# A decoder layer on one core: three quarters of the MLP's down projection as seven block products instead of eight, interleaved with the next up projections

## The chip, the core and the metric

The kernel runs on one core of a Trainium2 chip. The core has a matrix engine (TensorE, PE in the profile; its weight loads are PEld), a vector engine (VectorE, DVE), a scalar engine (ScalarE, ACT), a small general engine (GpSimd, POOL) and a queue engine (SyncE, SP) that issues most transfers from memory. Each engine works through its own list of instructions in order and waits for the others by semaphores. The metric is the device time of one execution in microseconds (us).

## What is computed

One layer: a normalised input projection, two token mixers, an output projection, then the MLP, then a gated side input. Only the MLP and its neighbours change:

```python
h  = h + rmsnorm(mixed @ w_o, g_post_mix)
v2 = rmsnorm(h, g_pre_mlp)
f  = jnp.square(jax.nn.relu(v2 @ w_up)) @ w_down      # w_up 1024x4096, w_down 4096x1024
h  = h + rmsnorm(f, g_post_mlp)
gate = jax.nn.sigmoid(rmsnorm(h, g_pre_ple) @ w_ple_gate + b_ple_gate)
h  = h + rmsnorm(gate * (p @ w_ple_in), g_post_ple)
```

There are 512 tokens (`S`), 1024 features (`D`) and 4096 hidden features (`FF`), all in 32-bit floats.

## The kernel before, in words

A matrix product of two 32-bit operands is made of three matmuls: each operand is split into a rounded part and the rest (`split`: ACT rounds, then DVE subtracts), and `PASSES` lists hi·hi, hi·lo, lo·hi. A matmul is 128x128 against 128x512.

Weights come in units of 256 rows by 512 columns (512 KB, one tile of the pool `pt`, 24 buffers, called `t`). `loads` fixes the order of the transfers on SP, `plan` the order in which `prep_next` splits units into the ring `w` of five buffers; `take` hands them to PE in the same order. A sixth unit is split only once the first has been used.

MLP before: the hidden features are cut into eight blocks of 512. `up()` computes one block as `gemm(4, feed(vT), ..., wstat=True)`: four units, 96 matmuls into four banks `a`, one for each 128 hidden features; ACT takes relu and square, DVE the rest of the split. Then for each half `n` of the output `gemm(2, list_feed(f_j), tok_out(facc, n, ...))` adds the block's share to `facc`: 48 matmuls for a half, 96 for a block. The order is up 0, up 1, down 0, up 2, down 1, and so on; the last block's down product is in the closing loop, which also makes the residual sum (`residual_features`: DVE, ACT, the power on POOL in `rstd`, then transposes `to_features` on PE).

The retention heads already use a seven-product form (`quartet`, Strassen-Winograd): a product of 2x2 blocks done as the products "11", 1, "12", 2, 4, 7, "22", whose operands are sums of the blocks. It has seven products of 24 matmuls in place of eight; `add_quartet` plans the sums of the weights.

`h1` (the residual, four tiles) and `e` (the side input's projection, two pairs of tiles) stay in the pool through the whole MLP. Tiles are written here as the listings print them: `t` pool tiles, `w` split weights, `u` the normalised, transposed activations (`vT`, `hT`), `s` half tiles, `a` and `b` banks, `st` and `rs` statistics.

Of the kernel before, what the change touches and what calls it, by code (L numbers as in the profile page):

```python
# [10 lines left out]
F32 = mybir.dt.float32  # L11
F32R = mybir.dt.float32r
# [12 lines left out]
MAGIC = 12582912.0  # L25
TWO_PI = (6.25, 17 / 512, -37 / 2 ** 21, 2 * math.pi - (6.25 + 17 / 512 - 37 / 2 ** 21))
PI_IN = 3.1415925
N_RAW, N_W, N_T, N_S = 4, 5, 24, 12


@with_exitstack
def hybrid_block(ctx, tc, a, out):
# [38 lines left out]
    def split(hi, lo, src):  # L71
        act(hi, src)
        tt(lo, src, hi.bitcast(F32), OP.subtract)
# [27 lines left out]
    def pop():  # L101
        if not raws:
            load_next()
        return raws.pop(0)
# [20 lines left out]
    def add_quartet(w, n1, n2):  # L125
        x, y, z = {}, {}, {}

        def first(k):
            x[k] = pop()
            return x[k]  # L130

        def add(a, b):
            tt(a, a, b, OP.add)
            return a

        def t1(k):
            y[k] = pop()
            return add(x[k], y[k])

        def t2(k):  # L140
            z[k] = pop()
            return add(x[k], z[k])

        for f, n, k0 in ((first, n1, 0), (t1, n2, 0), (lambda k: pop(), n1, 2), (t2, n2, 2),
                         (lambda k: z[k], None, 0), (lambda k: add(y[k], z[k]), None, 0),
                         (lambda k: add(x[k], pop()), n1, 2)):
            for k in range(2):
                if n is not None:
                    loads.append(w[n, k0 + k])
                plan.append(lambda f=f, k=k: f(k))  # L150

    w_in, w_ro, w_do = a["w_in"], a["w_ret_out"], a["w_dil_out"]
    for g in range(NG):
# [3 lines left out]
        add_units(w_in, c)  # L157
    for h in range(H):
        add_units(w_in, 3 * h)
        add_quartet(w_in, 3 * h + 2, 3 * h + 1)  # L160
    for n in range(2):
        add_units(w_do, n)
    for h in range(H):
# [3 lines left out]
        add_units(a["w_o"], n)  # L167
    add_units(a["w_ple_in"], 0)
    NFC = FF // 512
    add_units(a["w_up"], 0)  # L170
    for j in range(NFC):
        if j + 1 < NFC:
            add_units(a["w_up"], j + 1)
        for n in range(2):
            add_units(a["w_down"][j], n)
    add_units(a["w_ple_in"], 1)
# [172 lines left out]
    posr = half()  # L349

    def rotary(i):
        sc_i = const.tile([P, 2, S], F32, name="rot1") if i else big((P, 2, S))
# [275 lines left out]
    def quartet(lefts, c11, c12, c21, c22, early, late):  # L628
        def product(name, ps, first):
            for kk in range(2):  # L630
                w, = take(1)
                for t in range(2):
                    for k2 in range(2):
                        k = 2 * kk + k2
                        for q, (i, j) in enumerate(PASSES):
                            nc.tensor.matmul(ps[t], lefts[name](k, i, t), w[:, j, k2],  # L636
                                             start=(first and k == 0 and q == 0), stop=(k == 3 and q == 2),
                                             skip_group_check=not first)
# [4 lines left out]
        pa, pc = [abank() for _ in range(2)], [abank() for _ in range(2)]  # L643
        p1, q, u2 = ([half() for _ in range(2)] for _ in range(3))
        product("11", pa, True)
        for t in range(2):
            with tc.high_priority():
                act(p1[t], pa[t])
        product(1, pc, True)
        for t in range(2):  # L650
            with tc.high_priority():
                tt(q[t], pc[t], p1[t], OP.subtract)
        early()
        product("12", pa, False)
        for t in range(2):
            c11(t, pa[t])
        pb = [bank() for _ in range(2)]
        product(2, pb, True)
        for t in range(2):
            with tc.high_priority():  # L660
                tt(u2[t], pb[t], p1[t], OP.add)
        product(4, pc, False)
        for t in range(2):
            with tc.high_priority():
                tt(u2[t], pc[t], u2[t], OP.subtract)
            c12(t, u2[t])
        product(7, pb, False)
        for t in range(2):
            with tc.high_priority():
                tt(q[t], q[t], pb[t], OP.subtract)  # L670
            c22(2 + t, q[t])
        late()
        product("22", pb, False)
        for t in range(2):
            tt(p1[t], pb[t], p1[t], OP.add)
            c21(2 + t, p1[t])

    def rope_pair(x1, x2):
        res = []
# [14 lines left out]
    def head(h):  # L694
# [54 lines left out]
        def gate(t, br):  # L749
            stt(sg[t], br[0], br[1], sg[t])  # L750

        quartet(quads, g_evac, v_evac, g_inner, v_evac, scores,
                lambda: [gate(t, retain(t)) for t in range(2)])
        for t in (2, 3):
            gate(t, retain(t))

# [86 lines left out]
    pT32 = big((P, 2, 512))  # L843
    load(pT32, a["p"])
    pT = []
    for k in range(2):
        o = big((P, 2, 512), F32R)
        split(o[:, 0], o[:, 1], pT32[:, k])
        pT.append(o)

    g_post = bcast(a["g_post_mix"])
    g_pre = bcast(a["g_pre_mlp"])
# [10 lines left out]

    rs1 = const.tile([P, NT], F32, name="rs1")
    r0, ssq = {}, {}

    def wo_first(t, ps):
        ssq[t] = sumsq(ps)
# [19 lines left out]
    def e_evac(n):  # L888
        return lambda t, ps: act(at(e[n], t), ps)

    gemm(1, list_feed(pT), e_evac(0))
    flush()

    facc = [big() for _ in range(NT)]

    def up():
        fs = []

        def f(t, ps):
            r = half()  # L900
            act(r, ps, AF.Relu)
            o = big((P, 2, 512), F32R)
            act(o[:, 0], r, AF.Square)
            tt(r, r, r, OP.mult)
            tt(o[:, 1], r, o[:, 0].bitcast(F32), OP.subtract)
            fs.append(o)
        gemm(4, feed(vT), f, wstat=True)
        return fs
# [11 lines left out]
    rs2 = const.tile([P, NT], F32, name="rs2")  # L920
    us = take(4)
    hT = new_u()
    for t in range(NT):
        parts = []
        for n in range(2):
            ps = abank()
            acc_tile(ps, us[2 * n:2 * n + 2], list_feed(fs[NFC - 1]), t, False, prep_next if t == 3 else None)
            tok_out(facc, n)(t, ps)
            f = facc[t][:, halves[n]]
# [6 lines left out]
        residual_features(t, h1[t], r, g_pre2, rs2[:, t:t + 1], hT, [facc[t][:, sl] for sl in halves], 8)  # L936

    gemm(1, list_feed(pT), e_evac(1))
    flush()

    b_ple = bcast(a["b_ple_gate"])
# [107 lines left out]
```

## Time and profile before

| what | value |
|---|---|
| median of 3 runs | 1253.37 us (1252.58 to 1253.73) |
| the profiled execution's own time | 1251.57 us |
| its span, first to last instruction | 1249.8 us |
| TensorE busy | 1228.3 us, 98% of the span |
| VectorE busy | 746.2 us, 60% |
| ScalarE busy | 554.0 us, 44% |
| GpSimd busy | 50.3 us, 4% |

The span leaves 1.8 us of the profiled execution outside. The busy shares are means over stages; what counts is which engine a stage ends with. A matmul's recorded duration (about 390 ns) is longer than the step from one to the next, since matmuls overlap: a stretch's length divided by its matmuls gives the step.

### The profile page before, as it was taken

What the parts mean: (1) busy time and instruction counts of PE and PEld (TensorE: products, weight loads), DVE (VectorE), ACT (ScalarE), POOL (GpSimd) and SP (SyncE); (2) the same over time, 40 slices, a digit from 0 to 9 for tenths busy, and PEclk for the clock granted to TensorE, in tenths of its full rate; (3) what the DMA queues carried; (4) which work ended last, traced back from release to release, by engine and by line L of the source; (5) the groups of instructions that cost most, each with busy time, mean ns of one, the idle gap of its engine ahead of it and who ended that gap; (6) DMA issues with size and microseconds to landing.
All of it is one profiled execution on the core that took longest, in us unless ns stands there. A gap on an engine that the chain in (4) does not pass through costs nothing.

```text
span 1249.8 us, 15078 instructions
## 1 busy us (share of the span) xinstructions
PE 1228.3 (98%) x5708; PEld 1002.5 (80%) x5708; DVE 746.2 (60%) x1180; ACT 554.0 (44%) x926; POOL 50.3 (4%) x88
## 2 busy tenths in 40 slices
PE   7999999999999999999999999999999999999997
PEld 6877777877777888888888788878888888888886
DVE  6743644553369959769597267574344444354785
ACT  7334444446765535445355332353432233233462
POOL 1002011000010000000000000010000000000010
PEclk9999999999999999999999999999999999999999
DMA  9332233262316332423455343631222423232411
GB/s 339 136 106 72 66 91 112 60 202 70 116 60 227 114 124 92 143 84 135 135 185 200 114 176 120 251 118 34 71 81 86 133 84 101 85 117 72 149 51 68
DMA packets 51561, 149.43 MB, mean 120 GB/s; under 512 B 8352, under 2 KB 8608, under 8 KB 51488
## 3 DMA queue, kind: packets, MB, share of 16 engines
q1 hardware_dynamic: 41184, 133.91, 31.9%
q10 hardware_dynamic: 9024, 13.48, 3.4%
q0 software_dynamic: 1280, 1.08, 0.3%
q8 instruction: 45, 0.74, 0.2%
q14 instruction: 28, 0.23, 0.1%
HBM read 133.18 MB, written 11.53 MB: 116 GB/s over the span
## 4 chain that ended last, share of the span: by engine, by line
PE 92%; DVE 3%; DMA 2%; ACT 1%; issue 1%; POOL 0%; DVEq 0%; POOLq 0%; ACTq 0%
PE a L223 70%; PE a L636 7%; PE b L636 5%; PE b L454 2%; PE b L744 2%; PE b L484 2%; PE b L472 1%; DVE t L69 1%; PE b L729 1%; ACT s L66 1%; DMA t<-in_xT_dram 1%; DMA t<-in_x_dram 1%; DVE t L273 1%; PE b L760 0%; PE b L296 0%
## 5 line engine op out<-in xcount | busy, mean ns | idle before, releaser
L223 PE MATMUL a<-u,w 128*128 128x512 f32 x2112 | 506.7, 395 | 1.3 <-DVE s L69 0.9
L223 PEld LDWEIGHTS a<-u,w 128*128 128x128 f32 x2112 | 390.3, 188 | 87.0 <-issue 4.0
L66 ACT ACTIVATE w<-t 128x1024 fp32r<-128x1024 f32 (+1 forms) x230 | 238.6, 1044 | 263.7 <-PE a L223 187.8
L69 DVE TENSOR_TENSOR w<-t,w 128x1024 fp32r<-128x1024 f32 (+1 forms) x230 | 273.9, 1202 | 110.3 <-ACT w L66 107.7
L223 PE MATMUL a<-w,t 128*128 128x512 f32 x1008 | 231.7, 390 | 0.0
L223 PEld LDWEIGHTS a<-w,t 128*128 128x128 f32 x1008 | 188.8, 188 | 39.0
L69 DVE TENSOR_TENSOR t<-a,t 128x512 f32<-128x512 f32 x112 | 83.0, 743 | 96.4 <-PE a L223 65.0
L69 DVE TENSOR_TENSOR t<-t,t 128x512 f32<-128x512 f32 (+3 forms) x134 | 125.2, 955 | 3.9 <-ACT s L66 2.5
L223 PE MATMUL a<-w,u 128*128 128x512 f32 (+1 forms) x504 | 117.8, 389 | 5.0 <-ACT w L66 5.0
L223 PE MATMUL a<-t,w 128*128 128x512 f32 x480 | 110.5, 391 | 1.0 <-ACT t L66 0.6
L223 PEld LDWEIGHTS a<-w,u 128*128 128x128 f32 x504 | 91.5, 191 | 23.4 <-ACT w L66 5.0
L223 PEld LDWEIGHTS a<-t,w 128*128 128x128 f32 x480 | 89.8, 188 | 20.5 <-ACT t L66 1.3
L66 ACT ACTIVATE s<-b 128x512 f32<-128x512 f32 (+1 forms) x68 | 41.2, 612 | 93.9 <-PE b L472 40.0
L69 DVE TENSOR_TENSOR s<-s 128x512 f32<-128x512 f32 x32 | 22.2, 692 | 97.6 <-ACT t L66 97.6
L66 ACT ACTIVATE s<-a 128x512 f32<-128x512 f32 x48 | 28.5, 595 | 113.8 <-PE a L223 109.5
L458 DVE CUSTOM_DVE_ANT_0 s<-b,masks 128x128 f32<-128x128 f32 (+1 forms) x96 | 27.2, 320 | 85.8 <-PE b L454 85.7
L66 ACT ACTIVATE t<-a 80x512 f32<-80x512 f32 (+1 forms) x48 | 28.4, 591 | 57.8 <-PE a L223 46.3
L66 ACT ACTIVATE s<-s,st 128x128 f32<-128x128 f32 (+1 forms) x96 | 40.0, 418 | 26.6 <-DVE st L461 26.5
L284 POOL TENSOR_TENSOR st<-st,mhalf 128x1 f32<-128x1 f32 x28 | 15.7, 561 | 821.4 <-DVE st L282 821.4
L66 ACT ACTIVATE t<-s 128x512 fp32r<-128x512 f32 (+3 forms) x65 | 36.7, 588 | 23.6 <-DVE s L69 19.7
L636 PE MATMUL a<-w,u 128*128 128x512 f32 x192 | 45.1, 390 | 0.0
L636 PE MATMUL b<-w,t 128*128 128x512 f32 x192 | 44.8, 389 | 0.0
(108 smaller groups left out, 950.3 us busy)
## 6 DMA issues: line engine op xcount, KB each, us to landing
t<-in_w_in_dram SPq DMA_DIRECT2D x104, 512.0 KB
t<-in_w_up_dram SPq DMA_DIRECT2D x32, 512.0 KB
t<-in_w_down_dram SPq DMA_DIRECT2D x32, 512.0 KB
t<-in_w_ret_out_dram SPq DMA_DIRECT2D x16, 512.0 KB
t<-in_x_dram SPq DMA_DIRECT2D x8, 512.0 KB
zd<-s ACTq DMA_DIRECT2D x16, 256.0 KB
yrd<-s ACTq DMA_DIRECT2D x16, 256.0 KB
t<-zd SPq DMA_DIRECT2D x16, 256.0 KB
```

What stands on the lines that cost most here:

```text
L66: nc.scalar.activation(o, i, f, **kw)
L69: nc.vector.tensor_tensor(o, x, y, op=op)
L223: nc.tensor.matmul(ps, l, r, start=(k == 0 and q == 0), stop=(k == n - 1 and q == 2))
L273: return nc.vector.scalar_tensor_tensor(o, x, s, y, op0=op0, op1=op1)
L284: nc.gpsimd.tensor_tensor(r, v, mhalf[:, :1], op=OP.pow)
L454: nc.tensor.matmul(sb[hh][:, q * w:(q + 1) * w], at(qT, p0 + q)[rows, t * P:(t + 1) * P], at(kT, p0 + q)[rows, k0:k0 + w], start=True, sto ...
L458: nc.vector.tensor_tensor_reduce(out=sm[:, i, :], in0=sb[hh][:, q * w:(q + 1) * w], in1=mk, scale=1.0, scalar=NEG, op0=OP.add, op1=OP.max, ...
L472: nc.tensor.transpose(tb[:, c * P:(c + 1) * P], sm[:, i, j * P:(j + 1) * P], ident)
L484: nc.tensor.matmul(pv[:, s * HD:(s + 1) * HD], got["t"][:, c * P:(c + 1) * P], at(v, t - nb + 1 + j)[:, s * HD:(s + 1) * HD], start=(j == ...
L636: nc.tensor.matmul(ps[t], lefts[name](k, i, t), w[:, j, k2], start=(first and k == 0 and q == 0), stop=(k == 3 and q == 2), skip_group_che ...
L729: nc.tensor.matmul(b[:, :w], kT[d][:, i1, j * P:(j + 1) * P], qT[d][:, i2, j * P:], start=(n == 0), stop=(n == 5))
L744: nc.tensor.matmul(b, sc[j][:, i1, c:c + P], vh[j][:, i2, :], start=(n == 0), stop=(n == last))
```

## The change

For three chunks of 1024 hidden features (`NC = 3`) the down product is done in the seven-product form by `quartet`, now with its order, operands and outputs as arguments. After each product one unit of the next chunk's up projection follows (`up_unit`: 24 matmuls into four banks), two after the last. The hidden features of a chunk are kept as four unsplit quarters (`quarters`); `mix_in` makes the sums of quarters (DVE) and splits each (ACT, DVE). The last two blocks go the old way (`split_square`).

To make room, `h1` is written to memory by POOL's queue and read back before the closing loop; the first half of `e` is written by ACT's queue (`ed`) and read back by POOL's; `p` is loaded and split a second time (`side`). The pool `pt` has 25 buffers, one of which holds the rotary table `rot1` that was apart before.

```diff
-N_RAW, N_W, N_T, N_S = 4, 5, 24, 12
+N_RAW, N_W, N_T, N_S = 4, 5, 25, 12
...
+    EARLY, LATE = ("11", 1, "12", 2, 4, 7, "22"), ("11", 1, 2, 4, 7, "12", "22")
+    def add_quartet(quarter, order, between=()):
...
+        make = {
+            "11": ((0, 0), lambda k: keep(x, k)),
+            1: ((0, 1), lambda k: add(x[k], keep(y, k))),
+            2: ((1, 1), lambda k: add(x[k], keep(z, k))),
+            4: (None, lambda k: z[k]),
+            7: (None, lambda k: add(y[k], z[k])),
+            "12": ((1, 0), lambda k: pop() if again else keep(v, k)),
+            "22": ((1, 0) if again else None, lambda k: add(x[k], pop() if again else v[k])),
+        }
...
+    for c in range(NC):
+        ups = [(a["w_up"][2 * c + 2 + j, k], pop) for j in range(2) for k in range(4)]
+        add_quartet(lambda kh, nh, k, c=c: a["w_down"][2 * c + kh, nh, k], EARLY, ups)
...
+        for name in order:
+            if name in before:
+                before[name]()
...
+            for t in range(2):
+                with tc.high_priority():
+                    o = result(name, t)
+                if name in outs:
+                    outs[name](t, o)
...
+            if behind:
+                behind(name == order[-1])
...
+        nc.gpsimd.dma_start(h1d[t], h1[t])
...
-    e = {0: pair_tiles(), 1: pair_tiles()}
-    gemm(1, list_feed(pT), e_evac(0))
+    def e_first(t, ps):
+        x = half()
+        act(x, ps)
+        nc.scalar.dma_start(ed[t], x)
+
+    gemm(1, list_feed(pT), e_first)
...
+    def quarters():
+        o = [big((P, 4, 256)) for _ in range(2)]
+
+        def f(t, ps):
+            r = half()
+            act(r, ps, AF.Relu)
+            for x, sl in zip(o, (lo, hi)):
+                act(x[:, t], r[:, sl], AF.Square)
+        return o, f
...
-    fs = {0: up()}
-    for j in range(NFC - 1):
-        fs[j + 1] = up()
-        f_j = fs.pop(j)
-        for n in range(2):
-            gemm(2, list_feed(f_j), tok_out(facc, n, j == 0))
+    def down(c, f0, f1, following):
+        left = {}
+        a11, a21, a12, a22 = *f0, *f1
+        z = []
+
+        def mix_in(name):
+            if name == 1:
+                z.append(big((P, 4, 256)))
+                tt(z[0], a21, a22, OP.subtract)
+            elif name == 2:
+                tt(z[0], z[0], a11, OP.subtract)
+            elif name == 4:
+                tt(z[0], z[0], a12, OP.add)
+            elif name == 7:
+                tt(a21, a11, a21, OP.subtract)
+            src = {"11": a11, "12": a12, 7: a21, "22": a22}.get(name) if name not in (1, 2, 4) else z[0]
+            o = [big((P, 4, 256), F32R) for _ in range(2)]
+            split(o[0], o[1], src)
...
+            def add_to(t, n, x):
+                tt(part(t, n), x, part(t, n), OP.add)
...
+        def up_unit():
...
+            for t in range(4):
+                for k2 in range(2):
+                    k = 2 * kk + k2
+                    for n, (i, x) in enumerate(PASSES):
+                        nc.tensor.matmul(state["ps"][t], w[:, i, k2, t * P:(t + 1) * P], vT[:, x, k],
+                                         start=(k == 0 and n == 0), stop=(k == 7 and n == 2))
...
+    for t in range(NT):
+        nc.gpsimd.dma_start(h1[t], h1d[t])
...
+    pT = side()
+    e = {0: pair_tiles(), 1: pair_tiles()}
+    for t in range(NT):
+        nc.gpsimd.dma_start(at(e[0], t), ed[t])
+    gemm(1, list_feed(pT), lambda t, ps: act(at(e[1], t), ps))
```

PE in the first chunk. Before, a down block's last bank (a1230) is followed by a whole up projection, bank after bank, four units each (u1088 is `vT`):

```order
L223 MATMUL a1230_7166<-w1211_7025,t1181_6797 128x512 x3
L223 MATMUL a1230_7166<-w1211_7025,t1184_6828 128x512 x3
L223 MATMUL a1230_7166<-w1213_7036,t1187_6859 128x512 x3
L223 MATMUL a1230_7166<-w1213_7036,t1198_6910 128x512 x3
L223 MATMUL a1235_7190<-u1088_6436,w1215_7047 128x512 x6
L223 MATMUL a1235_7190<-u1088_6436,w1223_7107 128x512 x6
L223 MATMUL a1235_7190<-u1088_6436,w1225_7118 128x512 x6
L223 MATMUL a1235_7190<-u1088_6436,w1231_7173 128x512 x6
```

Now, at the end of product "12" (banks b1227 and b1228), one up unit goes through four banks, and product 2 begins in b1261, which takes the place in the pool that b1227 held:

```order
L686 MATMUL b1228_7083<-w1239_7150,t1225_7078 128x512 x2
L686 MATMUL b1228_7083<-w1239_7150,t1226_7079 128x512
L999 MATMUL a1235_7122<-u1089_6444,w1245_7174 128x512 x6
L999 MATMUL a1236_7123<-u1089_6444,w1245_7174 128x512 x6
L999 MATMUL a1237_7124<-u1089_6444,w1245_7174 128x512 x6
L999 MATMUL a1238_7125<-u1089_6444,w1245_7174 128x512 x6
L686 MATMUL b1261_7302<-w1247_7192,t1241_7156 128x512 x2
L686 MATMUL b1261_7302<-w1247_7192,t1242_7157 128x512
```

What moved: the up units stand between the products, and both banks of "12" have to be emptied within one up unit.

ACT where the up projections begin: before, three of `e`'s four banks (a1167 to a1169) are emptied ahead of a weight split (w1171), the sums of squares (s1158, s1160) and the last two pieces of `vT` (u1088):

```order
L66 ACTIVATE t1163_6711<-a1167_6715 128x512
L66 ACTIVATE t1163_6711<-a1168_6723 128x512
L66 ACTIVATE t1164_6712<-a1169_6731 128x512
L66 ACTIVATE w1171_6746<-t1142_6645 128x1024
L66 ACTIVATE s1158_6701,st1157_6700<-t1058_6281 128x512
L66 ACTIVATE s1160_6704,st1159_6703<-t1058_6281 128x512
L66 ACTIVATE u1088_6436<-b1173_6751 128x4x128
L66 ACTIVATE u1088_6436<-b1174_6758 128x4x128
L66 ACTIVATE t1164_6712<-a1170_6739 128x512
```

Now they stand behind the sums of squares, with the issues of their stores (ed), and ahead of `vT` (u1089):

```order
L66 ACTIVATE w1171_6760<-t1143_6656 128x1024
L66 ACTIVATE s1159_6712,st1158_6711<-t1059_6281 128x512
L66 ACTIVATE s1161_6715,st1160_6714<-t1059_6281 128x512
L66 ACTIVATE s1165_6730<-a1164_6723 128x512
L66 ACTIVATE s1167_6740<-a1166_6733 128x512
L921 DMA ed0_6300<-s1165_6730 128x512
L921 DMA ed1_6301<-s1167_6740 128x512
L66 ACTIVATE s1169_6750<-a1168_6743 128x512
L66 ACTIVATE u1089_6444<-b1173_6765 128x4x128
L921 DMA ed2_6302<-s1169_6750 128x512
L66 ACTIVATE u1089_6444<-b1174_6772 128x4x128
```

What moved: three emptyings of banks and two issues now come before the first of these two pieces of `vT`, and a third issue between them.

POOL in the closing loop: before, it has only the powers of the residual's statistics there:

```order
L284 TENSOR_TENSOR st1500_9042<-st1499_9040,mhalf_116 128x1
L284 TENSOR_TENSOR rs2_8852<-st1508_9059,mhalf_116 128x1
L284 TENSOR_TENSOR st1527_9136<-st1526_9134,mhalf_116 128x1
L284 TENSOR_TENSOR rs2_8852<-st1535_9153,mhalf_116 128x1
L284 TENSOR_TENSOR st1571_9384<-st1570_9382,mhalf_116 128x1
```

Now eight issues of transfers, four for `h1` (t1499 to t1502) and four for `e`, precede a tile's power (st1512):

```order
L1030 DMA t1499_8944<-h1d0_6296 128x1024
L1030 DMA t1500_8945<-h1d1_6297 128x1024
L1030 DMA t1501_8946<-h1d2_6298 128x1024
L1030 DMA t1502_8947<-h1d3_6299 128x1024
L1051 DMA t1589_9263<-ed0_6300 128x512
L1051 DMA t1589_9263<-ed1_6301 128x512
L1051 DMA t1590_9264<-ed2_6302 128x512
L1051 DMA t1590_9264<-ed3_6303 128x512
L294 TENSOR_TENSOR st1512_8993<-st1511_8991,mhalf_116 128x1
```

What moved: the first tile's power stands behind the issues for ed2 and ed3, whose target t1590 has the place of the reloaded `p` and is free once DVE has split it.

## Rows read from the trace of the kernel before

**Rows 1.** The page's head and its busy times by engine.

```profile
span 1249.8 us, 15078 instructions
...
PE 1228.3 (98%) x5708; PEld 1002.5 (80%) x5708; DVE 746.2 (60%) x1180; ACT 554.0 (44%) x926; POOL 50.3 (4%) x88
```

**Rows 2.** Chain that ended last, in order of time: start us, us, what.

```profile
404.19 10.88 PE a L636 x48
...
418.83 5.50 PE a L636 x24
...
838.48 336.99 PE a L223 x1485
1175.47 0.08 issue
1175.55 1.23 PE b L296 x8
...
1188.19 4.63 DMA t<-in_b_ple_gate_dram
```

**Rows 3.** Windows: heads, middle of the MLP, tail; busy us (instructions), clock, DMA.

```profile
core 0: us, PE busy (x) PEld busy (x) DVE busy (x) ACT busy (x) POOL busy (x), PEclk, DMA share, GB/s
384.00:680.00 296.00, 295.50 (x1359) 245.87 (x1360) 232.62 (x304) 144.28 (x206) 8.80 (x16) 1.00 0.41 139
...
921.00:1004.00 83.00, 83.00 (x368) 68.76 (x367) 40.12 (x48) 25.46 (x31) 0.00 (x0) 1.00 0.33 102
...
1175.00:1250.00 75.00, 65.14 (x323) 54.05 (x321) 54.79 (x102) 35.99 (x74) 9.01 (x11) 0.97 0.17 57
```

**Rows 4.** Groups by shape, 838 to 1175 us: count, busy us, mean ns, idle before.

```profile
L69 DVE TENSOR_TENSOR w<-t,w 128x1024 fp32r<-128x1024 f32 x61 | 74.2, 1222 | 38.6 <-ACT w L66 36.4
L66 ACT ACTIVATE w<-t 128x1024 fp32r<-128x1024 f32 x60 | 63.7, 1062 | 108.1 <-PE a L223 105.6 <-DVE t L69 1.8
L69 DVE TENSOR_TENSOR t<-a,t 128x512 f32<-128x512 f32 x50 | 34.4, 689 | 45.0 <-PE a L223 44.8
...
L66 ACT ACTIVATE s<-a 128x512 f32<-128x512 f32 x32 | 19.0, 593 | 101.3 <-PE a L223 101.3
```

**Rows 5.** Groups by shape, 384 to 680 us (the heads).

```profile
L69 DVE TENSOR_TENSOR t<-t,t 128x1024 f32<-128x1024 f32 x32 | 38.4, 1219 | 0.2
...
L66 ACT ACTIVATE t<-s 128x256 fp32r<-128x256 f32 x4 | 1.6, 402 | 0.0
```

**Rows 6.** Timeline of ACT and PE where the up projections begin.

```profile
834.69 1.06 ACT L66 ACTIVATE w<-t 128x1024 fp32r<-128x1024 f32 x1 [0.76 <-PE a L223]
...
836.27 0.61 ACT L66 ACTIVATE s<-t 128x512 f32<-128x512 f32 x1
...
836.88 1.06 ACT L66 ACTIVATE u<-b 128x512 fp32r<-128x512 f32 x2
...
837.51 2.71 PE L223 MATMUL a<-u,w 128*128 128x512 f32 x9 [0.41 <-ACT u L66]
```

**Rows 7.** Timeline of ACT and its queue where the last head's result is stored.

```profile
672.77 1.09 ACT L66 ACTIVATE s<-b 128x512 f32<-128x512 f32 x2
673.39 0.82 ACTq L763 DMA_DIRECT2D yrd<-s  x2
674.26 0.60 ACT L66 ACTIVATE s<-b 128x512 f32<-128x512 f32 x1 [0.40 <-ACT s L66]
```

**Rows 8.** Timeline of DVE and POOL in the closing loop, first tile.

```profile
1170.06 0.69 DVE L69 TENSOR_TENSOR t<-a,t 128x512 f32<-128x512 f32 x1 [0.45 <-PE a L223]
...
1172.61 0.55 POOL L284 TENSOR_TENSOR st<-st,mhalf 128x1 f32<-128x1 f32 x1 [333.19 <-DVE st L282]
...
1173.39 1.42 DVE L273 SCALAR_TENSOR_TENSOR t<-t,st,t 128x512 f32<-128x512 f32 x2
1174.72 1.28 DVE L69 TENSOR_TENSOR s<-t,t 128x512 f32<-128x512 f32 x2
```

**Rows 9.** Timeline of POOL and DVE later in the closing loop.

```profile
1192.87 2.35 DVE L69 TENSOR_TENSOR w<-t,w 128x1024 fp32r<-128x1024 f32 x2
1193.03 3.20 POOL L284 TENSOR_TENSOR rs<-st,mhalf 128x1 f32<-128x1 f32 x1 [5.81 <-DVE st L282]
```

**Rows 10.** POOL's issues of transfers of 32 rows, whole span.

```profile
L505 POOL DMA_DIRECT2D t<-t x16 | 8.6, 538 | 23.4 <-ACT t L66 23.3
```

More of the change, by code (lines that the diff above doesn't have):

```diff
@@ L123, in add_units, with keep @@
             plan.append(pop)
[L125 to L130, printed above, removed]
+    EARLY, LATE = ("11", 1, "12", 2, 4, 7, "22"), ("11", 1, 2, 4, 7, "12", "22")
+    def add_quartet(quarter, order, between=()):
+        x, y, z, v = {}, {}, {}, {}
+        again = order is EARLY
+        def keep(d, k):
+            d[k] = pop()
+            return d[k]
         def add(a, b):
@@ L134, in add @@
             return a
[L136 to L146, printed above, removed]
+        make = {
[8 more added lines that the diff above has]
+        for name in order:
+            src, f = make[name]
             for k in range(2):
-                if n is not None:
-                    loads.append(w[n, k0 + k])
+                if src is not None:
+                    loads.append(quarter(*src, k))
                 plan.append(lambda f=f, k=k: f(k))
+            for src, f in between[:1] if name != order[-1] else between:
+                loads.append(src)
+                plan.append(f)
+            between = between[1:]
     w_in, w_ro, w_do = a["w_in"], a["w_ret_out"], a["w_dil_out"]
@@ L626, in left_sums, with quartet, spare, place @@
         quads["22"] = lambda k, x, t: u[:, x, 4 + k, (2 + t) * P:(3 + t) * P]
-    def quartet(lefts, c11, c12, c21, c22, early, late):
-        def product(name, ps, first):
+    def quartet(order, left, outs, before={}, dest={}, behind=None):
+        pa, pb, pc, p1, q, u2 = ({} for _ in range(6))
+        group = {"11": pa, "12": pa, 1: pc, 4: pc, 2: pb, 7: pb, "22": pb}
+        def spare(d, t, to=None):
+            d[t] = half() if to is None else to
+            return d[t]
+        def place(name, t, own):
+            return dest[name](t) if name in dest else own
+        def result(name, t):
+            if name == "11":
+                act(spare(p1, t), pa[t])
+            elif name == 1:
+                tt(spare(q, t), pc[t], p1[t], OP.subtract)
+            elif name == 2:
+                tt(spare(u2, t), pb[t], p1[t], OP.add)
+            elif name == 4:
+                o = place(name, t, u2[t])
+                tt(o, pc[t], u2[t], OP.subtract)
+                return o
+            elif name == 7:
+                o = place(name, t, q[t])
+                tt(o, q[t], pb[t], OP.subtract)
+                return o
+            elif name == "22":
+                o = place(name, t, p1[t])
+                tt(o, pb[t], p1[t], OP.add)
+                return o
+            else:
+                return pa[t]
+        for name in order:
+            if name in before:
+                before[name]()
+            ps = group[name]
+            first = not ps
+            if first:
+                for t in range(2):
+                    ps[t] = bank() if behind or ps is pb else abank()
+            f = left[name]
             for kk in range(2):
@@ L641, in product @@
                         pump()
[L643 to L676, printed above, removed]
+            for t in range(2):
+                with tc.high_priority():
+                    o = result(name, t)
+                if name in outs:
+                    outs[name](t, o)
+            if name in ("12", "22"):
+                ps.clear()
+            if behind:
+                behind(name == order[-1])
     def rope_pair(x1, x2):
@@ L842, in hybrid_block, with side @@
         h1.append(x)
[L843 to L849, printed above, removed]
+    def side():
+        x = big((P, 2, 512))
+        load(x, a["p"])
+        res = []
+        for k in range(2):
+            o = big((P, 2, 512), F32R)
+            split(o[:, 0], o[:, 1], x[:, k])
+            res.append(o)
+        return res
+    pT = side()
     g_post = bcast(a["g_post_mix"])
@@ L865, in hybrid_block @@
     r0, ssq = {}, {}
+    h1d = [pdr.tile([P, D], F32, name=f"h1d{t}") for t in range(NT)]
+    ed = [pdr.tile([P, 512], F32, name=f"ed{t}") for t in range(NT)]
     def wo_first(t, ps):
@@ L916, in hybrid_block @@
+    fs = []
+    for j in range(2):
+        fs.append(quarters())
+        gemm(4, feed(vT), fs[j][1], wstat=True)
+    for c in range(NC):
+        nxt = [quarters() if c + 1 < NC else split_square() for _ in range(2)]
+        down(c, fs[0][0], fs[1][0], nxt)
+        fs = nxt
+    for n in range(2):
+        gemm(2, list_feed(fs[0][0]), tok_out(facc, n))
     g_post2 = bcast(a["g_post_mlp"])
@@ L935, in hybrid_block @@
             tt(r, r, rs1q[:, t:t + 1], OP.mult)
-        residual_features(t, h1[t], r, g_pre2, rs2[:, t:t + 1], hT, [facc[t][:, sl] for sl in halves], 8)
-    gemm(1, list_feed(pT), e_evac(1))
+        residual_features(t, h1[t], r, g_pre2, rs2[:, t:t + 1], hT, [part(t, n) for n in range(2)], 8)
+    pT = side()
+    e = {0: pair_tiles(), 1: pair_tiles()}
+    for t in range(NT):
+        nc.gpsimd.dma_start(at(e[0], t), ed[t])
+    gemm(1, list_feed(pT), lambda t, ps: act(at(e[1], t), ps))
     flush()
```

77 lines of the change are left out of this document (54 added, 23 removed).

## The prediction

> **What bounds the kernel now.** The page's busy times come first: PE is busy for 98% of the span, DVE for 60% and ACT for 44% [rows 1], so only work taken from PE, or a wait given to it, can move the end. Next I read the chain of waits in order of time. From 838.48 us it is one stretch of 336.99 us on PE with 1485 matmuls [rows 2], which is 0.227 us for each and leaves no room for a gap: neither DVE nor ACT nor a transfer sets the pace of the MLP. The heads, which already use the seven-product form, also lie in that chain, as 10.88 us for 48 matmuls and 5.50 us for 24 [rows 2]: again 0.227 us each, so a matmul in that form costs no more than another. The third view is busy time in windows. In the middle of the MLP DVE works 40.12 of 83 us and ACT 25.46, with a DMA share of 0.33; in the heads PE works 295.50 of 296 us beside a DVE that works 232.62 of them, 79% [rows 3]. The granted clock is 1.00 in both. The tail is less dense: PE works 65.14 of 75 us there [rows 3].
>
> **The change part by part.** *Fewer matmuls.* A chunk stands for two blocks of before: 192 matmuls of up and 192 of down. The seven products have 7 x 24 = 168 in place of 192, so three chunks lose 72 matmuls, and 72 x 0.227 = 16.3 us. A chunk is then 15 units of 24 matmuls, 5.45 us each (the chain's 5.50 for 24 agrees), 81.7 us on PE.
>
> *What DVE and ACT do in that time.* Per chunk DVE makes 22 remainders of split weights (14 of down, 8 of up), 8 sums of weights, 4 sums of quarters and 7 remainders of left operands: 41 operations of 1024 elements. The nearest rows are 1.222 us for a remainder [rows 4] and 1.219 for a sum [rows 5], so 41 x 1.22 = 50.0 us. To these come 10 operations that combine banks and 8 that add to `facc`, at 0.689 us each [rows 4]: 12.4 us. The sum is 62.4 of 81.7 us, 76%, against some half before; the heads carry 79% with a PE that doesn't wait, which is why I take the change of form itself as feasible. ACT has 29 roundings of 1.062 us, 8 relus of 0.593 [rows 4], 16 half squares of 0.402 (the row of 256 columns [rows 5]) and 2 copies of 0.6, 43 us in all: enough room.
>
> *Where a chunk is tight.* An average hides deadlines, so I followed the semaphores of the changed program. Let 0 be the moment at which a chunk's product "11" begins. The up unit before it fills four banks, 1.36 us each. (a) Its left operand hangs on the last up bank: the first half of the quarters is complete when the last relu and square have run, then round and remainder follow; along ACT and DVE in order, this gives about -0.4 us for the split's last part, against about 0.45 at which PE first wants the remainder (third matmul). About 0.85 us are left. (b) Product "12" ends one up unit before product 2, which takes over its banks' places (the order of PE above); the second bank's sum into `facc` must be out by 34.0 us. From 3.6 us, when the last square is done, DVE has 21 long and 4 short operations before it, 28.4 us at 1.22 and 0.689, so it is done between 32.0 and, with the waits that I count in between, 33.1. One to two us are left, and the recorded durations are on the long side: two long operations back to back take 2.35 us [rows 9]. (c) The rest of the chunk has several us to spare. So I take 0.1 us for a chunk, 0.3 for three; the bounds are 0 and 1 us a chunk, 3 in all, the latter if the listed operations each lose about 0.1 us to something that the rows of before don't show. In the first chunk the results of "12" go to ACT and this doesn't arise. The transfers in this stage: twelve reloads and the stores of `h1` add to a DMA share of 0.33, and the slots that they go to come free long before they are wanted.
>
> *The start of the up projections.* Before, ACT goes from a weight's rounding (834.69) over the sums of squares (836.27) to two pieces of `vT` (836.88), and PE waits 0.41 us for the first of them, at 837.51 [rows 6]. So ACT's order is on the path here. Now three emptyings of `e`'s banks and two issues of stores stand in front of the first piece, and a third issue ahead of the second. The nearest row is where the last head stores its results: two emptyings and two issues take from 672.77 to 674.26, 1.49 us [rows 7]; a third emptying adds 0.5. That is 2.0 us later, with bounds of 1.5 (the issues cover part of an emptying) and 2.5 (with the third issue, about 0.4 from the same row). Cover behind it there is none: PE has no other matmuls.
>
> *The tail.* POOL gets eight issues. The four of `h1` wait for places that come free before the loop and then have nothing behind them that is wanted soon. The issues for ed2 and ed3 wait until DVE has split the reloaded `p`, and the first tile's power is queued behind them on POOL. Before, that tile's last sum is made on DVE at 1170.06 and the power begins at 1172.61, 2.55 us later; DVE's two products follow at 1173.39, two sums at 1174.72, and PE's transposes at 1175.55 [rows 8], where the chain leaves 0.08 us of room [rows 2]. In the changed order DVE's split of `p` is done 1.2 to 1.65 us after that sum, so the two issues have about 1 us before they delay the power. POOL's only issues in the trace take 0.538 us each, but have 32 rows [rows 10]; these have 128. If rows don't matter, 2 x 0.54 fits and the delay is 0; if the time goes with rows, 2 x 2.15 = 4.3 us, 1.3 + 4.3 - 2.55 = 3.05 us late. With twice the time for four times the rows the two take 2.15, and the power comes 0.9 us late, which I take since the row's 32-byte and 2 KB transfers cost the same and so part of it is fixed; bounds 0 and 3.1. Who waits are DVE's two products and then the transposes, and behind those all that PE has left. `p` itself must come in again: a load that writes the same 512 KB (`b_ple_gate`) takes 4.63 us from issue to landing [rows 2], it is issued about 0.7 us ahead of the loop, and the first use lies 5.4 us into it, so it is in time by some 1.5 us.
>
> Here a lock bears on the issues. Row: one of POOL's powers took 3.20 us in place of 0.55 while DVE ran two operations that read two tiles of SBUF [rows 9]. The Trainium skill ("SBUF — State Buffer", section "Who interferes with whom") says that such a DVE instruction holds up a GpSimd instruction that reads SBUF, not one that only writes it, and infers that building descriptors needs the writing side; by that the issues would be untouched and the sum would stand. The trace of before has no POOL issue beside such an instruction, so it shows neither; the other answer is the third rival.
>
> *Sum:* -16.3 + 2.0 + 0.9 + 0.3 = -13.1 us. The profiled execution took 1251.57 (span 1249.8 and 1.8 outside) and becomes 1238.5; it lies 1.8 below the median of the three runs, so the median becomes **1240.3 us**. What lies outside the span should stay.
>
> **The rivals.** *DVE late twice a chunk.* If (a) and (b) each fail by 1.5 us, as they would if some 25 operations in a row took 0.1 us longer than their rows, the second and third chunk lose 3 us each: 1246.3. For it: slacks of 1 to 2 us on a sum of 28. Against: the heads at 79%, and pitches shorter than the recorded durations.
>
> *POOL slowed in the tail.* If each of the two issues is held like the power of [rows 9], they take 6.4 us: 1.3 + 6.4 - 2.55 = 5.15 us late in place of 0.9, so 1244.6. For it: DVE runs such operations at just that time, the power's row shows the lock; against: it is a single row, of another kind of instruction.
>
> *DVE becomes the bound (slower).* DVE works its list in order, and every product begins with an operand that it makes. If each of the 21 products' first matmul, or the up unit after it, waits for DVE, the saving is used up at (13.1 + 2.5) / 21 = 0.74 us a product; at 1 us a product the time is 1240.3 + 21 - 0.3 = 1261.0. For it: 62.4 us of work, with waits for PE, ACT and loads in the same list, and no slack that is seen by an average; against: the heads, where the same list in the same form costs PE 0.5 of 296 us.
>
> *No gain:* the saving goes into some waits of each kind, about 1253. Nothing in the views points to one of 13 us.
>
> **How the numbers follow.** About 0.2% (2.5 us) is what a measurement of this kernel can tell from no change. The forecast has a chance of 0.62, with its own range of 1237.5 (the start 1.5, no delay in the tail or a chunk, a little for the runs' own spread) to 1243.5 (the tail at 3.1 with the start at 2.5). DVE late has 0.17, POOL slowed 0.09, DVE as the bound 0.07, no gain 0.05. The range reaches to the second and third case, 1236.5 to 1247.5, and leaves out the slower half of DVE late and the last two. Faster by over 0.2% are the first three, 0.88; same 0.05; slower 0.07.
>
> **What would show it.** Right: in the chain, a stretch of PE with 72 fewer matmuls and 0.227 us each from the first up matmul on, some 321 us long; three emptyings between the sums of squares and `vT`, and the first up matmul 2 us after 837.51; a first transpose of the closing loop that waits about 1 us for DVE behind POOL's issues; DVE at about 76% of a chunk. Wrong: idle time of PE ended by DVE at the start of "11", or at product 2's second bank; POOL's issues longer than 1.1 us; or a matmul step over 0.227 us inside the quartets.

## The result and the profile after

The changed kernel takes **1240.18 us**, median of 4 runs (1239.32 to 1242.12), against 1252.97 before (1252.39 to 1253.73, 4 runs): ratio 0.990, 95% interval 0.9883 to 0.9917. The profiled execution took 1239.94 us. The page's head and its busy times, to be held against [rows 1]:

```profile
span 1238.1 us, 15113 instructions
PE 1213.0 (98%) x5636; PEld 990.2 (80%) x5636; DVE 803.7 (65%) x1215; ACT 593.1 (48%) x991; POOL 54.4 (4%) x100
```

PE has 72 matmuls less and is still busy for 98%; DVE has 57.5 us more work. The chain of waits of the changed kernel, in order of time (start us, us, what), from the first up matmul to the last of the three chunks and on to the closing loop:

```profile
838.98 0.49 ACT u L66
839.48 0.04 issue
839.52 45.55 PE a L233 x192
885.07 5.44 PE b L686 x24
890.51 5.44 PE a L999 x24
...
1113.55 5.44 PE b L686 x24
1118.99 10.88 PE a L999 x48
1129.87 29.93 PE a L233 x132
1159.80 0.03 issue
1159.83 1.07 POOL t L1051 x2
1160.90 0.02 issue
1160.91 0.58 POOL st L294
```

From 885.07 to 1129.87 us stand 45 units of 5.44 us and nothing else: 244.8 us for 1080 matmuls, 0.2267 each, as in the heads [rows 2]. No product and no up unit waits. Two other things are to be seen: the first two up blocks take 45.55 us for 192 matmuls, 2.0 more than 192 x 0.2267, and the chain leaves PE at 1159.80 for POOL.

The same stretch by windows (busy us and instructions of PE, PEld, DVE, ACT, POOL, then granted clock, DMA share, GB/s):

```profile
839.52:885.07 45.55, 45.55 (x193) 37.32 (x194) 11.64 (x11) 18.51 (x31) 0.00 (x0) 0.96 0.31 106
885.07:966.67 81.60, 81.60 (x361) 67.57 (x361) 55.97 (x53) 41.00 (x56) 0.00 (x0) 1.00 0.33 110
966.67:1048.27 81.60, 81.60 (x361) 67.57 (x361) 58.87 (x59) 40.30 (x56) 0.00 (x0) 1.00 0.34 116
1048.27:1129.87 81.60, 81.60 (x361) 67.57 (x361) 63.03 (x69) 40.02 (x49) 1.64 (x3) 1.00 0.45 155
```

Each chunk takes exactly its matmuls. DVE works 56 to 63 of 81.6 us (forecast 62.4), ACT 40 to 41 (forecast 43). The odd row is the first: a clock of 0.96. Finer windows where the up projections begin, changed kernel:

```profile
837.00:839.52 2.52, 0.11 (x1) 0.00 (x0) 1.47 (x5) 2.03 (x4) 0.56 (x1) 1.00 0.82 315
839.52:842.00 2.48, 2.48 (x5) 1.75 (x6) 1.37 (x2) 1.08 (x2) 0.00 (x0) 0.50 0.82 167
842.00:845.00 3.00, 3.00 (x12) 2.37 (x12) 0.00 (x0) 0.00 (x0) 0.00 (x0) 0.84 0.77 302
845.00:850.00 5.00, 5.00 (x23) 4.13 (x22) 0.00 (x0) 1.32 (x3) 0.00 (x0) 1.00 1.01 376
```

and the timeline of ACT and PE there (start us, us, engine, line, operation, then the idle time before it and what ended it):

```profile
834.69 1.06 ACT L66 ACTIVATE w<-t 128x1024 fp32r<-128x1024 f32 x1 [3.33 <-PE a L233]
835.88 1.23 PE L306 MATMUL b<-ident,s 128*128 128x128 f32 x8 [1.22 <-DVE s L69]
836.88 1.06 ACT L66 ACTIVATE s<-a 128x512 f32<-128x512 f32 x2
837.49 0.85 ACTq L921 DMA_DIRECT2D ed<-s  x2
838.38 0.60 ACT L66 ACTIVATE s<-a 128x512 f32<-128x512 f32 x1 [0.44 <-ACT s L66]
838.88 0.59 ACT L66 ACTIVATE u<-b 128x512 fp32r<-128x512 f32 x1
839.52 2.80 PE L233 MATMUL a<-u,w 128*128 128x512 f32 x5 [2.42 <-ACT u L66]
```

Where [rows 6] had the two pieces of `vT` at 836.88, there are now two emptyings, two issues and a third emptying; `vT` comes at 838.88 and PE has idled 1.22 and 2.42 us. Behind that its granted clock is 0.50, the lower of its two levels, and back at 1.00 by 845 us; the 0.84 is the mean of a window in which it rose.

The closing loop, first tile (DVE, ACT, POOL and PE), to be held against [rows 8]:

```profile
1150.98 0.33 SPq L82 DMA_DIRECT2D t<-in_p_dram  x1
...
1156.75 1.15 ACT L66 ACTIVATE t<-t 128x512 fp32r<-128x512 f32 x2 [0.82 <-DMA t<-in_p_dram]
1157.41 0.69 DVE L69 TENSOR_TENSOR t<-t,t 128x512 fp32r<-128x512 f32 x1 [0.76 <-ACT t L66]
1158.02 0.68 DVE L69 TENSOR_TENSOR t<-a,t 128x512 f32<-128x512 f32 x1
1158.62 0.68 DVE L69 TENSOR_TENSOR t<-t,t 128x512 fp32r<-128x512 f32 x1
...
1159.83 1.07 POOL L1051 DMA_DIRECT2D t<-ed  x2 [4.10 <-PE a L233]
1160.91 0.57 POOL L294 TENSOR_TENSOR st<-st,mhalf 128x1 f32<-128x1 f32 x1
...
1163.79 0.66 PE L306 MATMUL b<-ident,s 128*128 128x128 f32 x4 [1.05 <-DVE s L69]
```

DVE makes the first half of `p`'s remainder at 1157.41, since `p` has only just landed, 5.8 us after its issue, and the tile's last sum stands behind it, at 1158.02. The power follows that sum after 2.89 us, 0.34 more than the 2.55 of before. PE waits 1.05 us for the transposes. The second half of the split ends at 1159.30, 1.28 us after the sum began, and the issues for ed2 and ed3 start only 0.53 us later, at 1159.83. What holds them for that time stays open: this trace names PE as the releaser, the traces of six of the kernels below name DVE, and the distance is 0.52 or 0.53 us in all seven.

The difference of the two profiled executions, by three points that both have:

| stretch | before | after | difference |
|---|---|---|---|
| to the first up matmul | 837.51 | 839.52 | +2.01 |
| from there to the last matmul ahead of the first tile's transposes | 337.96 | 323.21 | -14.75 |
| wait ahead of these transposes | 0.08 | 1.06 | +0.98 |
| from them to the end of the span | 74.25 | 74.31 | +0.06 |

The sum is -11.7 us, the spans' difference. In the second row 71 matmuls are gone, 16.1 us (one stands behind the transposes now, in the fourth row), so 1.35 us were lost there; with that one matmul taken out, the fourth row lost 0.29.

### The profile page after: what moved, and what is told of

Its sections match the earlier page's. It is cut to its first block, busy times and chain, and to the rows that moved or that the text cites. A ratio compares the mean times of both kernels' runs of the same rounds, so it can differ in the third digit from the quotient of the medians.

```text
span 1238.1 us, 15113 instructions
## 1 busy us (share of the span) xinstructions
PE 1213.0 (98%) x5636; PEld 990.2 (80%) x5636; DVE 803.7 (65%) x1215; ACT 593.1 (48%) x991; POOL 54.4 (4%) x100
## 4 chain that ended last, share of the span: by engine, by line
PE 92%; DVE 3%; DMA 2%; ACT 2%; issue 1%; POOL 0%; DVEq 0%; POOLq 0%; ACTq 0%
PE a L233 50%; PE b L686 14%; PE a L999 11%; PE a L686 7%; PE b L464 2%; PE b L768 2%; PE b L494 2%; PE b L482 1%; DVE t L69 1%; ACT s L66 1%; PE b L753 1%; DMA t<-in_xT_dram 1%; DMA t<-in_x_dram 1%; DVE t L283 1%; PE b L306 1%
## 5 line engine op out<-in xcount | busy, mean ns | idle before, releaser
L69 DVE TENSOR_TENSOR w<-t,w 128x1024 fp32r<-128x1024 f32 (+1 forms) x248 | 296.1, 1204 | 158.2 <-ACT w L66 156.0
L69 DVE TENSOR_TENSOR t<-t,t 128x1024 f32<-128x1024 f32 (+4 forms) x193 | 194.4, 1031 | 23.5 <-ACT t L66 18.3
L686 PE MATMUL b<-w,t 128*128 128x512 f32 x696 | 162.5, 389 | 0.0
L686 PEld LDWEIGHTS b<-w,t 128*128 128x128 f32 x696 | 130.6, 188 | 27.1
L233 PE MATMUL a<-w,t 128*128 128x512 f32 x432 | 100.5, 391 | 0.0
L233 PEld LDWEIGHTS a<-w,t 128*128 128x128 f32 x432 | 80.6, 188 | 16.5
L69 DVE TENSOR_TENSOR t<-a,t 128x512 f32<-128x512 f32 x72 | 55.6, 773 | 58.2 <-ACT t L66 30.2
L66 ACT ACTIVATE t<-t 128x512 fp32r<-128x512 f32 (+1 forms) x61 | 45.5, 770 | 38.3 <-DVE t L69 36.6
L69 DVE TENSOR_TENSOR s<-a,t 128x512 f32<-128x512 f32 x40 | 26.4, 687 | 38.7 <-PE a L233 31.4
L66 ACT ACTIVATE t<-s 128x256 f32<-128x256 f32 (+3 forms) x90 | 39.1, 481 | 23.3 <-DVE s L69 19.7
```

Of the source, the lines that this page charges most:

```text
L233: nc.tensor.matmul(ps, l, r, start=(k == 0 and q == 0), stop=(k == n - 1 and q == 2))
L686: nc.tensor.matmul(ps[t], f(k, i, t), w[:, j, k2], start=(first and k == 0 and n == 0), stop=(k == 3 and n == 2), skip_group_check=not first)
```

## The experiments

Each kernel is the changed one with the edit shown; the runs of before beside them have medians of 1251.67 us (14 runs; first four kernels), 1252.31 (7; the next four) and 1252.28 (7; the last two). Beside the changed kernel it was 1252.97, so the medians of one kernel differ by up to 1.3 us from one set of runs to the next, and a difference of about a microsecond between two kernels is read from their traces.

**The start repaired (vt_first).** The side input's banks go to two big tiles, and SP stores them.

```diff
+    e0 = pair_tiles()
     def e_first(t, ps):
-        x = half()
+        x = at(e0, t)
         act(x, ps)
-        nc.scalar.dma_start(ed[t], x)
+        nc.sync.dma_start(ed[t], x)
```

> The four banks of the side input's projection are emptied into two big tiles and stored through SP's queue, so that ACT's order where the up projections begin is that of the kernel before: sums of squares, the two last pieces of vT, then the fourth emptying. Theory (wait and clock): the changed kernel's first up matmul is 2.0 us late, and since PE has idled 2.4 us, its granted clock drops to 0.50 and 0.84 in the next 5 us, which costs 1.75 us more. Both go: first up matmul at about 837.5 us, clock 1.00 behind it, the time 3.8 us below the changed kernel, 1236.4 us. Rival (wait alone): the slow first matmuls wait for DVE's remainders of vT and stay slow: 2.0 us below, 1238.2 us.

Measured: 1236.52 us (1235.72 to 1237.14), ratio 0.9876 (0.986 to 0.9892), 3.7 below the changed kernel. Its timeline has ACT's old order and PE's old wait:

```profile
836.50 0.61 ACT L66 ACTIVATE s<-t 128x512 f32<-128x512 f32 x1
837.11 1.06 ACT L66 ACTIVATE u<-b 128x512 fp32r<-128x512 f32 x2
837.74 10.65 PE L233 MATMUL a<-u,w 128*128 128x512 f32 x44 [0.41 <-ACT u L66]
838.06 0.59 ACT L66 ACTIVATE t<-a 128x512 f32<-128x512 f32 x1
```

The granted clock is 1.00 in all windows behind it, and the first two up blocks take 44.2 us (837.74 to 881.93). So of the 3.7 us, 2.0 are the wait and 1.36 (45.55 less 44.19) what came with it; the rest is a shorter wait in the tail (0.61 in place of 1.05), against transposes that begin 0.22 us later here (836.10, 835.88 in the changed kernel). These sum to 3.6, the difference of the two profiled spans (1238.1 and 1234.5).

**PE kept busy through the wait (pe_warm).**

```diff
+    idle = bank()
+    for i in range(14):
+        nc.tensor.matmul(idle[:, :384], ready[0][:, 0, 0, :P], vT[:, 0, 0, :384], start=True, stop=True)
```

> The changed kernel with 14 extra matmuls of 384 columns, whose result nobody reads, on PE between the last transposes and the first up matmul; ACT's order and DVE's remainders stay as they are, so the first up matmul still begins at about 839.5 us. Theory (wait and clock): with PE kept busy the granted clock stays at 1.00, the first two up projections take about 43.8 us in place of 45.55, and the time falls by 1.75 us to 1238.4 us. Rival (wait for the remainders): the 192 matmuls take 45.5 us as before, the time stays at 1240.2 us.

Measured in the trace: ACT is as late as before (`vT` at 839.02), PE's first up matmul stands at 839.66, and the chain and the windows show

```profile
837.25 2.46 PE b L927 x14
839.71 43.81 PE a L233 x192
```

```profile
839.66:842.00 2.34, 2.34 (x11) 1.84 (x11) 1.34 (x2) 1.09 (x2) 0.00 (x0) 1.00 0.57 205
```

43.8 us as the clock theory has it: the first up matmul isn't earlier, DVE's remainders aren't either, and the slow matmuls are gone. So the trace shows the price of the clock. The times don't: the profiled execution took 1238.94, but the median is 1240.38 (1238.94 to 1240.51), where 1238.4 was expected. Part was given back in the closing loop, where PE waits 1.61 us in place of 1.05 for the first tile, because `p` landed 6.3 us after its issue. What the other three runs lost can't be read, since only one is profiled.

**No chunk and one chunk in the new form (chunks0, chunks1).** `NC` is set to 0 and to 1; the remaining blocks go through the old loop, and everything is stored and read back as in the changed kernel.

```diff
-    NC = NFC // 2 - 1
+    NC = 0
...
+    for j in range(2 * NC, NFC - 1):
+        for n in range(2):
+            gemm(2, list_feed(fs[0][0]), tok_out(facc, n, j == 0))
```

> The changed kernel without any chunk in the seven-product form: all eight blocks go the old way, while h1, e and p are still stored and read back. Theory (the terms add): 72 matmuls of 0.227 us come back, 16.3 us, and the cost of making room stays, so 1240.2 + 16.3 = 1256.5 us, slower than the kernel before by about 3.5 us. Rival (making room is free, and a chunk saves less than its matmuls): about 1253 us, as before.

> The changed kernel with one chunk in place of three in the seven-product form. Theory (the terms add): two chunks less, 48 matmuls of 0.227 us, 10.9 us: 1251.1 us, and the chunk itself lasts 81.6 us. Rival (the first chunk alone runs without waits, since its results go to ACT, and the others hide a loss): a time above 1251.1 by less or more than 1 us, with idle time of PE in one of the three chunks of the changed kernel.

Measured: 1256.80 us (1255.13 to 1258.94), ratio 1.0037 (1.0024 to 1.005), and 1251.68 us (1249.37 to 1253.87, 10 runs), ratio 0.9999 (0.999 to 1.0009). From the first up matmul to the end the spans have 415.05 and 409.83 us against 398.58 with three chunks: 16.5 and 11.25 us for 72 and 48 matmuls, where 16.3 and 10.9 were expected. (Two things that differ from one execution to the next are in the 16.5: with no chunk the clock is still at 0.59 from 841.35 to 844.35, and the first tile's transposes wait 0.49 us in place of 1.05.) The one chunk of the second kernel takes 81.6 us (886.87 to 968.47). So the terms add, and making room alone makes the kernel slower by some 5 us (1256.80 less 1251.67; the terms for the start, the clock and the tail below sum to 4.6). With one chunk the two effects cancel.

**More work for DVE in each chunk (dve_plus1, dve_plus2).** The remainder of each left operand is made once or twice more.

```diff
             split(o[0], o[1], src)
+            for _ in range(1):
+                tt(o[1], src, o[0].bitcast(F32), OP.subtract)
```

> The changed kernel with the remainder of each product's left operand made twice on DVE (the same numbers again): seven more operations of about 1.15 us in each chunk, 63 + 8 = 71 of 81.6 us. Theory (deadlines): the left operand of product 11 is 0.93 us early in the changed kernel's trace and becomes 0.2 us late in three chunks; the second bank of product 12 is emptied about 3.5 us early, and with four more operations ahead of it it is about 1 us late in the second and third chunk: 0.6 + 2.0 = 2.6 us, 1242.8 us, with idle time of PE at these two places alone. Rival (average): DVE still has 10 us to spare in a chunk, so the time stays at 1240.2 us.

> The same with two repeats: fourteen more operations of about 1.15 us, 63 + 16 = 79 of 81.6 us. Theory (deadlines): product 11 1.4 us late in three chunks, the second bank of product 12 about 5.7 us late in two: up to 15.6 us, about 1255 us, slower than the kernel before. Rival (average): DVE's work still fits in a chunk, 1240.2 us, or a few tenths more.

Measured: 1239.82 us (1239.56 to 1243.0) and 1242.36 us (1241.26 to 1244.65). By the time the first is a draw with the changed kernel, and not the 2.6 us slower that I had expected; the trace tells more. With one repeat the chain has all units at 5.44 us but two:

```profile
966.86 5.67 PE b L686 x24
1037.81 10.88 PE a L1001 x48
1048.69 5.67 PE b L686 x24
```

These are product "11" of the second and third chunk, each 0.23 us late, as the deadline said (0.2); in the first chunk, where I had expected the same, nothing is late. The second bank of "12" is not late: its sum ends 30.4 us after the chunk's start in the changed kernel, 31.6 with one repeat (997.11 + 1.30 - 966.86), and is wanted at 34.0. With two repeats it ends at 1003.61 (1002.92 + 0.69), and that isn't late either, for product 2 begins behind 29 up matmuls in place of 24 and wants the bank 1.36 us after its start, at 1003.87:

```profile
995.94 6.57 PE a L1001 x29
1002.51 5.44 PE b L686 x24
```

In the first 30 us of the second chunk DVE's windows read, for the changed kernel and with one and two repeats:

```profile
966.67:996.67 30.00, 30.00 (x134) 24.82 (x134) 27.32 (x26) 16.87 (x21) 0.00 (x0) 1.00 0.26 88
```

```profile
966.86:996.86 30.00, 30.00 (x133) 24.55 (x133) 29.15 (x27) 16.93 (x21) 0.00 (x0) 1.00 0.27 87
```

```profile
968.66:998.66 30.00, 29.94 (x132) 24.48 (x131) 29.93 (x28) 16.49 (x20) 0.00 (x0) 1.00 0.26 88
```

So DVE is at 91% there in the changed kernel, and full with two repeats; what I hadn't counted as slack is the idle time that the extra work fills, and that other work moved behind the sum: with one repeat the window has one operation more, not four. The three chunks then take 245.7 us in place of 244.8, far from the 15 us that I had expected: when the program with two repeats was built, some up matmuls were put between those of a product, which covers part of the waits, so the second deadline stays untested. The rest of its 2.2 us lies ahead of the chunks and of the first repeat: the first up matmul is 0.4 later, and the first two up blocks take 46.72 us, as the clock is still at 0.50 from 842.41 to 845.41. With one repeat they take 46.37 us, with 0.56 from 841.39 to 844.39.

**The reloads of e on SP (ed_on_sp), and p held back (tail_clean).**

```diff
-        nc.gpsimd.dma_start(at(e[0], t), ed[t])
+        load(at(e[0], t), ed[t])
```

```diff
+        if after is not None:
+            nc.vector.tensor_copy(x[:, 0, :1], after)
         load(x, a["p"])
...
-    pT = side()
+    pT = side(h1[0][:, :1])
```

The second kernel has both edits.

> The changed kernel with the four reloads of e's first half issued by SP in place of POOL; the reload of p stays. Theory (p): POOL's two issues of 0.54 us delay the first tile's power by only 0.33 us, and what remains of the wait is DVE's, which has the split of the reloaded p ahead of the tile's last sum; the PE idles about 0.7 us ahead of that tile's transposes in place of 1.05, and the time falls by 0.3 us. Rival (the term of the prediction): the issues cost the whole 0.9 us, and it goes.

> The changed kernel with the reloads of e on SP and the reload of p held back until the first tile's residual sum is made (one copy of one column on DVE sets that order), so that the split of p stands behind that tile's work. Theory (p): PE idles at most 0.2 us ahead of the first tile's transposes in place of 1.05, the time falls by about 0.9 us to 1239.3 us, if p's later split delays no later tile. Rival (POOL alone): no more than with the reloads on SP; or p now comes late for its own product, and the time rises.

Measured: 1240.71 us (1239.55 to 1242.75) and 1240.08 us (1239.71 to 1240.47), no change in either. With the reloads on SP, the power comes 2.48 us after the tile's last sum in place of 2.89, but PE still waits 0.99 us, because `p` landed 6.1 us after its issue and DVE made the sum that much later. With `p` held back too, the first tile's transposes don't wait at all, and nothing is won:

```profile
1162.62 1.26 PE L306 MATMUL b<-ident,s 128*128 128x128 f32 x8
...
1181.10 1.23 PE L306 MATMUL b<-ident,s 128*128 128x128 f32 x8 [0.38 <-DVE s L69]
...
1191.31 0.63 PE L306 MATMUL b<-ident,s 128*128 128x128 f32 x4 [0.35 <-DVE s L69]
```

Waits of 0.38 and 0.35 us now stand at the third and fourth tile, where the changed kernel has none and 0.60. From the end of the last chunk to the end of the span it is 108.2 us in both (1129.87 to 1238.1, 1130.03 to 1238.2). My expectation that the time would fall by 0.9 us was wrong: I now take it that not the order of DVE's work in the loop counts but its amount, which the next kernel tests. Between the first and the last tile of the changed kernel DVE is nearly as full as PE, 28.92 of 31 us against 29.35, while ACT has 19.87:

```profile
1160.00:1191.00 31.00, 29.35 (x142) 23.87 (x140) 28.92 (x57) 19.87 (x43) 4.77 (x9) 1.00 0.20 68
```

**p asked for ahead of the loop (p_early), and both repairs (start_and_p).** `side()` is called ahead of the last plain down block, so that the split of `p` is done by the time the loop begins; e's reloads are on SP. The second kernel has the repaired start as well.

```diff
+    pT = side()
     for n in range(2):
         gemm(2, list_feed(fs[0][0]), tok_out(facc, n))
...
-    pT = side()
     e = {0: pair_tiles(), 1: pair_tiles()}
```

> The changed kernel with the second load and split of p asked for ahead of the last plain down block instead of behind the closing loop, and with e's reloads on SP, so that neither stands in DVE's or POOL's order between the first tile's last sum and its transposes. Theory (DVE bounds the closing loop, 29.9 of 32 us, and the two remainders of p's split are 1.2 us of it): the stretch from the last chunk's end to the kernel's end falls from 108.2 us to about 107.0, the time to 1239.0 us; holding p's split back inside the loop gained nothing for that reason. Rival (only the first tile's wait counts): that wait of 1.05 us goes, as it did when p was held back, but the end stays, 1240.1 us.

> Both repairs: the order of ACT at the start of the up projections as before the change (stores of e through SP) and the early p with e's reloads on SP. If the terms add: 3.7 us from the start (2.0 wait, 1.4 clock, 0.3 of the tail) and about 1 us from the tail, 1235.5 us, faster than the changed kernel by 4.7 us and than the kernel before by about 17 us. If the tail takes back what the start gives: no faster than the run with the start repaired alone, 1236.5 us.

Measured: 1239.38 us (1238.78 to 1239.94), and **1235.85 us** (1235.43 to 1237.08), ratio 0.9869 (0.9852 to 0.9885). With the early `p`, the last stretch is 106.9 us (1130.57 to 1237.5), 1.3 less, as the amount of DVE's work asked. The first tile's transposes don't wait, and from them to the fourth tile's it is 27.05 us, as before the change (27.02; 27.21 in the changed kernel). The median is 0.8 lower, which the medians alone can't tell from nothing (in the profiled execution the first up matmul came 0.7 later). Both repairs together are 4.3 us faster than the changed kernel (3.9 by the profiled spans, 1238.1 and 1234.2) and 16.4 faster than before: nearly what the 72 matmuls are worth. Against the start repaired alone the early `p` gives 0.6 us in the last stretch (107.2 after 107.8), since there `p` had landed early enough to leave a wait of only 0.61.

## Why the prediction was right, step by step

The forecast was 1240.3 us, the result 1240.18, and the mechanism was the likeliest case's. That it agrees to 0.1 us is luck: the sum gave -13.1 for the profiled executions, which differ by -11.6, so the terms were 1.5 us too low in all. I had added 1.8 us for the median, and the execution profiled after lay only 0.2 below its median, which happens to make up the difference. (One rival's time has a slip: 1246.3 holds the 0.3 and the 6 us that replace it, so 1246.0.)

- **Fewer matmuls, -16.3 us:** right. 0.2267 us each in the chain, and 16.5 when all are put back (chunks0).
- **A chunk's deadlines, +0.3:** 0. Slack (a) was 0.93 us (remainder done at 966.19, wanted at 967.12) against 0.85, and the 0.23 us lost with one repeat shows that this deadline is real; slack (b) was 3.6 us against 1 to 2, and no run made it fail.
- **The start, +2.0:** the wait is 2.01 us, but the term was too small: 3.4. I priced the wait and not what PE does after it. The granted clock of 0.50 and 0.84 costs 1.36 us more, shown from two sides: by the repaired start, and by matmuls put into the wait. Against the matmuls put into the wait it is 1.74 (45.55 less 43.81). Nor is it a fixed price: behind the same wait of 2.42 us the two blocks took 46.37 and 46.72 us in the kernels with one and two repeats. That the views of before showed 1.00 there said nothing on this, as PE's wait for `vT` was 0.41 us [rows 6].
- **The tail, +0.9:** 1.27 (0.98 and 0.29), of other parts than I named, so that 0.98 is near 0.9 is luck. POOL's issues cost 0.54 us each, not 1.07: four times the rows take no longer. By my own sum they would have fitted (1.28 + 1.07 in 2.55); the power is 0.34 us late since they start 0.53 us after the split's end, which I had not foreseen. In the working, the step that failed is "it is in time by some 1.5 us": `p` takes 5.1 to 6.3 us to land in these runs, not 4.63, and its two remainders go into a loop in which DVE has little room. In the six kernels that keep this order of DVE and POOL, PE's wait ahead of the first tile is the landing time less 4.7 us, from 0.50 us (landed after 5.19) to 1.61 (6.31); with the reloads of `e` on SP it is 0.99 after 6.11, 0.4 less. I read DVE's share for the chunks and not for the tail, where [rows 3] already had 54.79 us of DVE beside 65.14 of PE.
- **The rule weighed there:** the first of the two issues ran beside a DVE operation with two SBUF inputs (1159.67 to 1160.36), and the two took 1.07 us, 0.535 each, as without one, so the lock of [rows 9] doesn't hold for it. The Trainium skill ("SBUF — State Buffer", section "Who interferes with whom") says that such an instruction holds up GpSimd's reads, not its writes, and infers that building descriptors needs the writing side; this trace agrees. The rival "POOL slowed" is out.
- **DVE late, or DVE as the bound:** out for this kernel, and not near. With one repeat DVE took 7 us more a chunk, and the three chunks 0.46 us more in all (885.26 to 1130.52).

## What to carry to other kernels

A wait of the bounding engine has a second price: behind a wait of 2.42 us in place of 0.41, the matmuls ran at half clock for some us, and the wait and its echo were repaired by one edit. Before costing work at nothing in a stage with slack, ask which engine is fullest in the stage that it lands in, and whether its order or its amount counts: moving `p`'s split within the closing loop moved the wait, taking it out of the loop removed it. A deadline by deadline reading predicted the 0.2 us at product "11" where the busy share of 76% predicted nothing; at product "12" it predicted waits that didn't come.

## What I had not expected of the hardware

PE's clock fell after waits of 1.22 and 2.42 us with 1.2 us of transposes between them, and not after 1.21 and 0.41. For how long it stayed at 0.50 differed from run to run. A load of 512 KB took between 5.1 and 6.3 us from issue to landing at the same place of eight kernels, and PE waited for it in all eight. POOL issued a transfer of 128 rows of 2 or 4 KB in 0.53 to 0.59 us, about the time of one of 32 rows [rows 10].
